# Prompt attention of a hybrid decoder step: other points of the projection for transposes, softmax and values, and the next input made two points later

## The chip, the cores and the metric

The kernel runs on one core of one Trainium2 chip. Time is device time in microseconds; lower is better. TensorE (PE) multiplies, VectorE (DVE) and ScalarE (ACT) read its results out of PSUM, GpSimd (POOL) helps out and issues some of the transfers, SyncE (SP) issues the rest.

## The reference

One layer of a decoder on 2048 prompt positions and 32 sample positions, width 1024, float32. What the change touches is the prompt's token mixing: one input projection, then two kinds of windowed attention on its columns.

```python
qa, ka, va, qb, kb, vb, ga, gb = _project(x, w_in)          # x @ w_in
qa, ka, qb, kb = _rope(qa, pos), _rope(ka, pos), _rope(qb, pos), _rope(kb, pos)
# A: 8 query heads on 2 key heads, window 128, blocks of 128, a learned sink per head
s = _band_scores(qa.reshape(...), ka, A_WINDOW)
p = _sink_softmax(s, _sink_logits(sink_a))
oa = _band_values(p, va)
# B: three groups of 4 heads, (window, dilation) = (128,1), (512,4), (2048,16)
for g, (win, dil) in enumerate(B_DIL):
    qg, kg, vg = (_stride_split(z[:, :, hs], dil) for z in (qb, kb, vb))
    p, lse = _softmax_lse(_band_scores(qg, kg, win // dil))
    outs.append(_band_values(p, vg))
# then: merge of the groups, gates, output projection, layer norm, gated ConvFFN, layer norm
```

Band scores of a block of 128 queries run over the keys of its own block and of the one before it.

## The kernel before

The program has three phases: projection with attention (to about 1320 us of the span), gates with output projection (to about 1710), and the ConvFFN. The change lies in the first.

**Precision.** Every float32 operand of a product is split in a high and a low part (`split`: ACT copies the high part, DVE or POOL subtracts to get the low one), and a product is three matmuls.

**Slots.** Phase 1 is a list `seq` of slots. The kinds are B0, B1, B2 (the three groups of B), A, and G (gates). Each kind has 16 slots of 128 prompt positions and one for the samples (slot 16; it comes last except in G). B0 and A take positions in order, B1 with stride 4, B2 with stride 16. In B2, and in every fourth slot of B1, a block has no block before it, so it has 128 keys and not 256.

**Points.** A slot multiplies its input `xs` (128 positions, both parts, eight k) with four units of weights of 256 columns, in two halves of two units; each half fills one PSUM tile `psd` of a pool with two tiles. After each half of a unit, that is after 12 matmuls of line 379, `adv()` lets every running attention job take one step: eight points a slot, numbered 0 to 7 here. The jobs are generators; each `yield` ends a step. The attention of a block starts in the slot after its projection. So the order of the program is written by hand, by where the `yield`s stand, and every engine works its instructions off in that order.

**Around the points.** `late()` reads the q/k half out of PSUM at point 5 in B and point 4 in A (`rope`: L425, L426, L433 on DVE), and the other half at the end of the slot (the gate's columns on ACT, L449). `prep` makes the input of the next slot: in B0 it loads and transposes x (L335) and copies it to `R` (L336 on ACT); in all it splits `xs` out of `R` (L41 on ACT, then L42 on DVE, or on POOL in A). It stands after unit 0, that is after point 1 (in the first slot of B0, B1 and B2 after point 3). `adv_bg` gives DVE a pair of instructions for the samples' scores (L797, L800) after point 2 and after point 6 in B; there are 16 such pairs for each group: in slots 2 to 9 of B1 and of B2, and from slot 2 to slot 13 of A. `adv_w` splits new weights near a change of kind.

**A job of B** (`attn_b`) transposes q (L630) and k (L634), splits them (`split_q`, `split_k`), splits v out of the PSUM tile (`split_v`), makes scores (`qk`, L617 and L619), the softmax of two pairs of heads (`softmax_pair`: maxima L546 on DVE, `nm` L550, exponentials L552 on ACT), transposes P (`transpose_p`, L562, then its split), multiplies with the values (L659) and adds the two parts of the result (`both`: L570 on ACT, L571 on DVE). A job of A (`attn_a`) does the same for two halves r of its heads.

Of the kernel before, what the change touches and what calls it, by code (L numbers as in the profile page):

```python
# [34 lines left out]
class Net:  # L35
# [254 lines left out]
    def adv(self):  # L290
        for j in self.jobs[::-1]:
            try:
                next(j)
            except StopIteration:
                self.jobs.remove(j)
# [56 lines left out]
    def slot(self, kind, i, t, xs, units, prep, after_unit, rp):  # L352
# [13 lines left out]
        for half in range(2):  # L366
            ps = self.pd.tile([128, 512], F32, tag="d", name="psd")
            for uu in range(2):
# [20 lines left out]
                if u == (1 if kind[0] == "B" and i == 0 else 0):  # L389
# [151 lines left out]
    def softmax_pair(self, sps, nk, mask, m, nm, den, cols, accum=True, init=None):  # L541
# [8 lines left out]
        nc.vector.tensor_scalar(nm[:, csl], m[:, csl], -SCALE, None, ALU.mult)  # L550
# [71 lines left out]
    def attn_b(self, kind, i, t):  # L622
# [6 lines left out]
        for p in range(2):  # L629
            nc.tensor.transpose(ps[:, p * 128:(p + 1) * 128], q[:, p * 128:(p + 1) * 128], self.idn)  # L630
        qT = self.split_q(ps[:, 0:256].rearrange("p (r t) -> p r t", r=2))
        ps = self.psO.tile([128, 512], F32, tag="o", name="pst")
        for p in range(2):
            nc.tensor.transpose(ps[:, p * 128:(p + 1) * 128], kv[:, p * 128:(p + 1) * 128], self.idn)  # L634
        self.split_k(ps[:, 0:256].rearrange("p (r t) -> p r t", r=2), i % 2)
        yield
        v = self.split_v(self.vps)
        vprev, self.vprev = self.vprev, v
        yield
# [4 lines left out]
        nc.gpsimd.dma_start(self.d_md[g, rows, :], md)  # L644
        yield
        vs = [v] if nb == 1 else ([v, vprev] if swap else [vprev, v])
        PTs = []
        yield
        for x in range(2):
            yield  # L650
            PTs.append(self.transpose_p(Ps[x], [(c, b) for c in range(2) for b in range(nb)]))
        O = self.buf()
        for x in range(2):
            yield
# [11 lines left out]
    def attn_a(self, t):  # L666
# [15 lines left out]
        yield  # L682
        m = self.at.tile([128, 8], F32, tag="m8", name="m8")
# [5 lines left out]
        def softmax(r, x, sps):  # L689
# [8 lines left out]
            nc.vector.tensor_scalar(nm[:, c:c + 2], m[:, c:c + 2], -SCALE, None, ALU.mult)  # L698
# [11 lines left out]
        def values(r, x, PT):  # L710
            for b in range(nb):
                for q in range(2):
                    nc.tensor.matmul(ops[:, r * 256:(r + 1) * 256], lhsT=vs[b][:, x], rhs=PT[:, q, b * 256:(b + 1) * 256],
                                     start=(b == 0 and q == 0), stop=(b == nb - 1 and q == 1))

        def out(x):
            o = self.both(O, ops, x)
            nc.gpsimd.dma_start(self.d_oa[x * 256:(x + 1) * 256, rows].rearrange("(h d) t -> d h t", h=4),
                                o.rearrange("p (h t) -> p h t", h=4))
# [913 lines left out]
```

## Time and profile before

| | us |
|---|---|
| median of 3 runs | 3258.62 (3256.92 to 3259.58) |
| profiled execution | 3259.99 |
| its span | 3258.2 |
| mean granted TensorE clock | 0.994 |

The page gives busy time by engine, waits by who waited for whom, and groups of instructions; times are microseconds from the span's start. A row of the timeline has start, length, engine, line, operation, output and inputs, and in brackets the idle time before it with what ended it. Matmuls overlap in the pipeline, so the distance from start to start says what one costs, not its own length. In the tables by stage the columns are: length, busy time of PE, PEld (weight loads), DVE, ACT and POOL with their counts, granted clock, share of the DMA engines and GB/s.

### The profile page before, as it was taken

The numbers are of one execution on the slowest core, as the hardware profiler recorded it, in microseconds if no ns is written. First come the engines' busy times: TensorE is split into PE (matmuls) and PEld (weight loads), VectorE is DVE, ScalarE is ACT, GpSimd is POOL, SyncE is SP. The second block draws the span as 40 slices with busy tenths as digits, with TensorE's granted clock in tenths as the row PEclk, the third lists the DMA queues.
The fourth block names the chain that finished last, engine by engine and source line by source line (L and its number), as shares of the span: only waits on it lengthen the run. The fifth ranks groups of instructions, "written<-read, shape, count | busy, mean of one in ns | idle before, by whom it ended". The sixth has DMA issues, their size and how long they took to land.

```text
span 3258.2 us, 56718 instructions
## 1 busy us (share of the span) xinstructions
PE 3175.0 (97%) x21839; PEld 2907.4 (89%) x21839; DVE 1947.6 (60%) x4030; ACT 1397.0 (43%) x3097; POOL 565.5 (17%) x671
## 2 busy tenths in 40 slices
PE   8999999999999899899999999999999999999999
PEld 8998999999899899788877988888888888999998
DVE  5667877877887632577765444564446444574446
ACT  6666656665666533412224243342243332342332
POOL 2112112223121200255540000030002100030001
PEclk9999999999999999999999999999999999999999
DMA  3113212412221343876744323443334423443231
GB/s 116 56 47 95 82 31 86 121 63 89 79 57 38 91 131 98 227 194 175 187 131 140 121 84 101 127 142 91 95 100 120 139 86 101 120 138 91 69 95 57
DMA packets 480036, 343.02 MB, mean 105 GB/s; under 512 B 113938, under 2 KB 435564, under 8 KB 479766
## 3 DMA queue, kind: packets, MB, share of 16 engines
q1 hardware_dynamic: 462390, 290.78, 31.5%
q0 software_dynamic: 17232, 48.56, 4.8%
q8 instruction: 172, 2.82, 0.4%
q14 instruction: 98, 0.80, 0.1%
q10 hardware_dynamic: 144, 0.07, 0.0%
HBM read 279.71 MB, written 59.59 MB: 104 GB/s over the span
## 4 chain that ended last, share of the span: by engine, by line
PE 58%; issue 2%; DMA 2%; DVE 1%; SPq 0%; ACT 0%; POOL 0%; DVEq 0%; POOLq 0%; ACTq 0%
PE psu L1392 31%; PE psdn L1070 14%; PE psw L1070 5%; PE psb L1070 4%; PE psd L379 2%; PE psdf L1070 1%; DMA oa<-d_oa 1%; PE pst L1234 0%; PE pso L964 0%; PE pst L1269 0%; DMA ob<-d_ob 0%; DMA ga<-d_gate 0%; DMA b<-in_w_o 0%; SPq L1126 0%; DMA b<-in_w_br_b 0%
## 5 line engine op out<-in xcount | busy, mean ns | idle before, releaser
L1392 PE MATMUL psu<-h,w 128*128 128x512 f32 (+1 forms) x5280 | 1013.6, 354 | 2.2 <-ACT h L41 2.0
L379 PE MATMUL psd<-w,xs 128*128 128x256 f32 x7680 | 1001.1, 285 | 8.7 <-ACT w L41 4.0
L1392 PEld LDWEIGHTS psu<-h,w 128*128 128x128 f32 x5280 | 861.2, 188 | 149.0 <-ACT h L41 3.4
L379 PEld LDWEIGHTS psd<-w,xs 128*128 128x128 f32 x7680 | 945.7, 190 | 12.9 <-ACT w L41 4.4
L1070 PE MATMUL psdn<-w,gt 128*128 128x256 f32 (+1 forms) x4008 | 474.9, 279 | 2.2 <-DVE y L1443 2.2
L1070 PEld LDWEIGHTS psdn<-w,gt 128*128 128x128 f32 (+1 forms) x4008 | 472.2, 186 | 5.3 <-DVE y L1443 4.5
L42 DVE TENSOR_TENSOR w<-b,w 128x512 fp32r<-128x512 f32 (+1 forms) x613 | 403.7, 717 | 21.4 <-ACT w L41 20.4
L41 ACT ACTIVATE w<-b 128x512 fp32r<-128x512 f32 x636 | 346.5, 607 | 127.4 <-PE psdn L1070 64.2
L1403 ACT ACTIVATE ext<-psu 128x512 f32<-128x512 f32 (+1 forms) x110 | 56.3, 512 | 452.2 <-PE psu L1392 452.1
L1416 DVE SCALAR_TENSOR_TENSOR ac<-ext,cw,ac 128x512 f32<-128x512 f32 (+1 forms) x88 | 71.1, 808 | 286.9 <-ACT ac L1415 286.9
L1443 DVE SCALAR_TENSOR_TENSOR y<-y,psdn 128x256 f32<-128x256 f32 x176 | 73.2, 420 | 274.2 <-PE psdn L1070 270.4
L1070 PE MATMUL psw<-WO,mT 128*128 128x512 f32 (+1 forms) x800 | 189.4, 395 | 0.9 <-DVE mT L42 0.9
L1070 PEld LDWEIGHTS psw<-WO,mT 128*128 128x128 f32 (+1 forms) x800 | 148.5, 186 | 38.9 <-DVE mT L42 1.1
L1412 POOL COPY mix<-ext 128x2 f32<-128x2 f32 x66 | 13.0, 196 | 926.5 <-ACT ext L1403 906.4
L42 DVE TENSOR_TENSOR xs<-R,xs 128x1024 fp32r<-128x1024 f32 x64 | 104.8, 1638 | 114.9 <-ACT xs L41 114.8
L1070 PE MATMUL psb<-w,oT 128*128 128x512 f32 (+1 forms) x600 | 147.6, 404 | 7.7 <-ACT b L449 5.0
L41 ACT ACTIVATE gt<-ac 128x512 fp32r<-128x512 f32 x110 | 58.3, 549 | 222.2 <-DVE ac L1423 162.7
L1070 PEld LDWEIGHTS psb<-w,oT 128*128 128x128 f32 (+1 forms) x600 | 112.4, 190 | 36.3 <-ACT b L449 5.7
L552 ACT ACTIVATE P<-P,nm 128x256 f32<-128x256 f32 (+1 forms) x192 | 86.4, 451 | 123.1 <-issue 87.4
L42 DVE TENSOR_TENSOR PT<-pst,PT 128x512 fp32r<-128x512 f32 (+1 forms) x160 | 96.2, 608 | 66.6 <-ACT PT L41 66.0
L662 POOL TENSOR_TENSOR b<-b 64x256 f32<-64x256 f32 x96 | 71.3, 742 | 337.4 <-DVE b L571 337.4
L41 ACT ACTIVATE xs<-R 128x1024 fp32r<-128x1024 f32 x80 | 116.2, 1452 | 0.9 <-ACT b L756 0.4
(257 smaller groups left out, 3679.1 us busy)
## 6 DMA issues: line engine op xcount, KB each, us to landing
b<-in_w_up SPq DMA_DIRECT2D x352, 256.0 KB, 3.9
b<-in_w_down SPq DMA_DIRECT2D x160, 256.0 KB, 3.4
b<-in_w_in SPq DMA_DIRECT2D x80, 256.0 KB, 4.1
b<-in_x_prompt SPq DMA_DIRECT2D x64, 256.0 KB, 4.0
b<-in_cache_b SPq DMA_DIRECT2D x64, 256.0 KB, 3.3
ga<-d_gate SPq DMA_DIRECT2D x32, 512.0 KB, 5.4
b<-d_q SPq DMA_DIRECT2D x48, 256.0 KB, 3.9
d_gate<-b SPq DMA_DIRECT2D x64, 128.0 KB, 1.9
```

What stands on the lines that cost most here:

```text
L41: self.nc.scalar.activation(hi, src, AF.Copy)
L42: (eng or self.nc.vector).tensor_tensor(lo, src, hi.bitcast(F32), ALU.subtract)
L379: nc.tensor.matmul(dst, lhsT=l, rhs=r[:, k, :], start=(k == 0 and q == 0), stop=(k == 7 and q == len(ops) - 1))
L552: nc.scalar.activation(P[:, x, :nk], P[:, x, :nk], AF.Exp, bias=nm[:, c:c + 1], scale=SCALE, accum_out=den[:, c:c + 1])
L662: nc.gpsimd.tensor_tensor(o[:, :, 0], o[:, :, 0], o[:, :, 1], ALU.add)
L1070: self.nc.tensor.matmul(ps[:x.shape[1]], lhsT=x, rhs=w, start=(first and q == 0), stop=(last and q == len(ops) - 1))
L1392: nc.tensor.matmul(ps[:, :b1 - b0], lhsT=w[:, k, c0:c0 + 128], rhs=h[:, x, k, b0:b1], start=(k == 0 and q == 0), stop=(k == 7 and q == 2))
L1403: nc.scalar.activation(ext[:, 2 + b0:2 + e1], ps[:, 0:e1 - b0], AF.Copy)
L1412: nc.gpsimd.tensor_copy(carry[:, j, :], ext[:, W:W + 2])
L1416: nc.vector.scalar_tensor_tensor(ac[:, :L], ext[:, 1:1 + L], cw[:, 1, j:j + 1], ac[:, :L], ALU.mult, ALU.add)
L1443: nc.vector.scalar_tensor_tensor(y[x][:M, cs], y[x][:M, cs], ALPHA if first else 1.0, ps[:M], ALU.mult, ALU.add)
```

## The change

The order in which jobs take their step is turned round: the older job first. The steps move:

- B: q and k are transposed into one PSUM tile at point 0 (k was in the one tile of pool `psO`); v is split at point 2 and not 1; scores and softmax come at point 3 and not 2; both P are transposed at point 0 of the slot after (they had points 5 and 6), directly ahead of the new block's q and k; both value products come at point 2 of that slot (they had point 7 and point 0).
- A: first scores and softmax at point 3 and not 2, P's transposes in pairs at point 5 and at point 0 of the next slot (they had points 4, 6, 9 and 8), values for half the heads at point 7 and at point 2 of the next slot, in one PSUM tile each; the result goes out in four transfers a slot and not two, of half the size.
- `prep` stands after unit 1, that is after point 3, in all prompt slots of B and A.
- `nm` (the maxima times -SCALE) is made by ACT and not by DVE.

Three places show how it moves instructions. DVE in a slot of B1 without a pair for the samples (row `ISA P` is one maximum, `ISA md` its read-out; `vr` is the split of v, `PT` the split of P). Before:

```order
L443 TENSOR_TENSOR vr<-psd,vr 128x2x64 x2
L42 TENSOR_TENSOR xs<-R,xs 128x1024
L546 ISA P,md<-pss,mk 128x256
...
L550 TENSOR_SCALAR nm<-md 128x2
L42 TENSOR_TENSOR PT<-pst,PT 128x512
L425 TENSOR_TENSOR q<-psd,cs 128x256
L425 TENSOR_TENSOR kv<-psd,cs 128x256
L426 TENSOR_TENSOR b<-psd,cs 128x512
```

After:

```order
L443 TENSOR_TENSOR vr<-psd,vr 128x2x64 x2
L546 ISA P,md<-pss,mk 128x256
...
L546 ISA md 128x1
L42 TENSOR_TENSOR xs<-R,xs 128x1024
L425 TENSOR_TENSOR q<-psd,cs 128x256
L425 TENSOR_TENSOR kv<-psd,cs 128x256
L426 TENSOR_TENSOR b<-psd,cs 128x512
L433 TENSOR_TENSOR q<-q,b 128x256
L433 TENSOR_TENSOR kv<-kv,b 128x256
L42 TENSOR_TENSOR PT<-pst,PT 128x512 x2
```

The split of xs stood ahead of the four maxima; now it stands behind them, directly ahead of the rotation that reads `psd`, and both splits of P follow the rotation. ACT in a slot of B0, before:

```order
L570 ACTIVATE b<-pso 64x512
L440 ACTIVATE vr<-psd 128x2x64 x2
L336 ACTIVATE R<-pst 128x4x128 x2
L41 ACTIVATE xs<-R 128x1024
L552 ACTIVATE P,md<-P,nm 128x256 x4
L41 ACTIVATE PT<-pst 128x512 x2
```

After:

```order
L570 ACTIVATE b<-pso 64x512 x2
L440 ACTIVATE vr<-psd 128x2x64 x2
L550 ACTIVATE nm<-md 128x2
L552 ACTIVATE P,md<-P,nm 128x256 x2
L550 ACTIVATE nm<-md 128x2
L552 ACTIVATE P,md<-P,nm 128x256 x2
L336 ACTIVATE R<-pst 128x4x128 x2
L41 ACTIVATE xs<-R 128x1024
```

The copies to R and the high part of xs moved behind the exponentials, and nm came in ahead of each pair. PE in a slot of B0, from the first block of a slot on, before:

```order
L379 MATMUL psd<-w,xs 128x256 x12
L630 MATMUL pst<-idn,q 128x128 x2
L634 MATMUL pst<-idn,kv 128x128 x2
L659 MATMUL pso<-PT,vr 128x256 x4
L379 MATMUL psd<-w,xs 128x256 x12
L335 MATMUL pst<-idn,b 128x128 x8
L379 MATMUL psd<-w,xs 128x256 x12
```

After:

```order
L562 MATMUL pst<-idn,P 128x128 x8
L630 MATMUL pst<-idn,q 128x128 x2
L630 MATMUL pst<-idn,kv 128x128 x2
L379 MATMUL psd<-w,xs 128x256 x24
L655 MATMUL pso<-PT,vr 128x256 x8
L379 MATMUL psd<-w,xs 128x256 x12
L617 MATMUL pss<-kH_378,qT 128x256
```

All twelve transposes of P, q and k stand together behind the first block, the eight value products two blocks later, and the scores one block after these. The diff (context cut):

```diff
@@ -288,7 +288,7 @@
                 self.bgq.pop(0)
 
     def adv(self):
-        for j in self.jobs[::-1]:
+        for j in list(self.jobs):
             try:
                 next(j)
             except StopIteration:
@@ -386,7 +386,7 @@
                         self.adv_w(pace[2 * u + kh])
                     if (u, kh) == (1, 0) or ((u, kh) == (3, 0) if kind != "A" else (u, kh) == (2, 0) and i < 6):
                         self.adv_bg()
-                if u == (1 if kind[0] == "B" and i == 0 else 0):
+                if u == (0 if kind == "G" or smp else 1):
                     out = prep()
                     if kind == "G" and i == 14:
                         rp.close()
@@ -547,7 +547,7 @@
                 out=P[:, x, :nk], in0=sps[:, x * 256:x * 256 + nk], in1=mask, scale=1.0,
                 scalar=NEG if init is None else init[:, c:c + 1], op0=ALU.add, op1=ALU.max, accum_out=m[:, c:c + 1])
         csl = slice(cols[0], cols[1] + 1, cols[1] - cols[0])
-        nc.vector.tensor_scalar(nm[:, csl], m[:, csl], -SCALE, None, ALU.mult)
+        nc.scalar.activation(nm[:, csl], m[:, csl], AF.Copy, scale=-SCALE)
         for x, c in enumerate(cols):
             nc.scalar.activation(P[:, x, :nk], P[:, x, :nk], AF.Exp, bias=nm[:, c:c + 1], scale=SCALE,
                                  accum_out=den[:, c:c + 1])
@@ -626,32 +626,28 @@
         sl, mask, nb, swap = self.keys(i, has_prev)
         nk = nb * 128
         ps = self.psT.tile([128, 512], F32, tag="t", name="pst")
-        for p in range(2):
-            nc.tensor.transpose(ps[:, p * 128:(p + 1) * 128], q[:, p * 128:(p + 1) * 128], self.idn)
+        for p in range(4):
+            nc.tensor.transpose(ps[:, p * 128:(p + 1) * 128], (q, kv)[p // 2][:, p % 2 * 128:(p % 2 + 1) * 128], self.idn)
         qT = self.split_q(ps[:, 0:256].rearrange("p (r t) -> p r t", r=2))
-        ps = self.psO.tile([128, 512], F32, tag="o", name="pst")
-        for p in range(2):
-            nc.tensor.transpose(ps[:, p * 128:(p + 1) * 128], kv[:, p * 128:(p + 1) * 128], self.idn)
-        self.split_k(ps[:, 0:256].rearrange("p (r t) -> p r t", r=2), i % 2)
+        self.split_k(ps[:, 256:512].rearrange("p (r t) -> p r t", r=2), i % 2)
+        yield
         yield
         v = self.split_v(self.vps)
         vprev, self.vprev = self.vprev, v
+        vs = [v] if nb == 1 else ([v, vprev] if swap else [vprev, v])
         yield
         md = self.at.tile([128, 8], F32, tag="m8", name="md")
         nm = self.at.tile([128, 8], F32, tag="nm", name="nm")
         sps = self.qk(qT, sl, nk, ((0, 0), (1, 1)))
         Ps = [self.softmax_pair(sps[x], nk, mask, md[:, 0:4], nm, md[:, 4:8], (x, 2 + x)) for x in range(2)]
         nc.gpsimd.dma_start(self.d_md[g, rows, :], md)
-        yield
-        vs = [v] if nb == 1 else ([v, vprev] if swap else [vprev, v])
-        PTs = []
-        yield
-        for x in range(2):
+        for _ in range(5):
             yield
-            PTs.append(self.transpose_p(Ps[x], [(c, b) for c in range(2) for b in range(nb)]))
+        PTs = [self.transpose_p(P, [(c, b) for c in range(2) for b in range(nb)]) for P in Ps]
+        yield
+        yield
         O = self.buf()
         for x in range(2):
-            yield
             ops = self.psT.tile([128, 512], F32, tag="t", name="pso") if x else self.psO.tile([128, 512], F32, tag="o", name="pso")
             for c in range(2):
                 for b in range(nb):
@@ -680,6 +676,7 @@
         self.split_k(pk[:, None, 0:128], i % 2)
         yield
         yield
+        yield
         m = self.at.tile([128, 8], F32, tag="m8", name="m8")
         nm = self.at.tile([128, 8], F32, tag="nm", name="nm")
         den = self.denA[:, i]
@@ -695,7 +692,7 @@
                 nc.vector.tensor_tensor_reduce(out=P[:, y, :nk], in0=sps[x][:, y * 256:y * 256 + nk], in1=mask, scale=1.0,
                                                scalar=self.sk8[:, c + y:c + y + 1], op0=ALU.add, op1=ALU.max,
                                                accum_out=m[:, c + y:c + y + 1])
-            nc.vector.tensor_scalar(nm[:, c:c + 2], m[:, c:c + 2], -SCALE, None, ALU.mult)
+            nc.scalar.activation(nm[:, c:c + 2], m[:, c:c + 2], AF.Copy, scale=-SCALE)
             for y in range(2):
                 nc.scalar.activation(P[:, y, :nk + 1], P[:, y, :nk + 1], AF.Exp, bias=nm[:, c + y:c + y + 1], scale=SCALE,
                                      accum_out=den[:, c + y:c + y + 1])
@@ -707,44 +704,35 @@
         def trans(P):
             return self.transpose_p(P, [(y, b) for b in range(nb) for y in range(2)])
 
-        def values(r, x, PT):
-            for b in range(nb):
-                for q in range(2):
-                    nc.tensor.matmul(ops[:, r * 256:(r + 1) * 256], lhsT=vs[b][:, x], rhs=PT[:, q, b * 256:(b + 1) * 256],
-                                     start=(b == 0 and q == 0), stop=(b == nb - 1 and q == 1))
-
-        def out(x):
-            o = self.both(O, ops, x)
-            nc.gpsimd.dma_start(self.d_oa[x * 256:(x + 1) * 256, rows].rearrange("(h d) t -> d h t", h=4),
-                                o.rearrange("p (h t) -> p h t", h=4))
+        def values(r, PTs):
+            ops = self.psO.tile([128, 512], F32, tag="o", name="pso")
+            for x in range(2):
+                for b in range(nb):
+                    for q in range(2):
+                        nc.tensor.matmul(ops[:, x * 256:(x + 1) * 256], lhsT=vs[b][:, x],
+                                         rhs=PTs[x][:, q, b * 256:(b + 1) * 256],
+                                         start=(b == 0 and q == 0), stop=(b == nb - 1 and q == 1))
+            o = self.both(self.buf(), ops, r)
+            for x in range(2):
+                h0 = (4 * x + 2 * r) * 64
+                nc.gpsimd.dma_start(self.d_oa[h0:h0 + 128, rows].rearrange("(y d) t -> d y t", y=2),
+                                    o[:, x * 256:(x + 1) * 256].rearrange("p (y t) -> p y t", y=2))
 
         sps = scores(0)
-        P0, P1 = softmax(0, 0, sps), softmax(0, 1, sps)
-        yield
-        yield
-        t0 = trans(P0)
+        Ps = [softmax(0, x, sps) for x in range(2)]
+        yield
+        yield
+        PTs = [trans(P) for P in Ps]
         sps = scores(1)
-        P0 = softmax(1, 0, sps)
-        yield
-        ops = self.psO.tile([128, 512], F32, tag="o", name="pso")
-        values(0, 0, t0)
-        yield
-        t0 = trans(P0)
-        yield
-        P0 = softmax(1, 1, sps)
-        yield
-        values(1, 0, t0)
-        O = self.buf()
-        out(0)
-        t0 = trans(P1)
-        yield
-        t1 = trans(P0)
-        yield
-        ops = self.psO.tile([128, 512], F32, tag="o", name="pso")
-        values(0, 1, t0)
-        yield
-        values(1, 1, t1)
-        out(1)
+        Ps = [softmax(1, x, sps) for x in range(2)]
+        yield
+        yield
+        values(0, PTs)
+        yield
+        PTs = [trans(P) for P in Ps]
+        yield
+        yield
+        values(1, PTs)
 
     def store_rec(self):
```

## The prediction

> **What bounds the kernel now.** I read the page first, then busy time by stage, then one slot of each kind on TensorE (PE), VectorE (DVE) and ScalarE (ACT), and last the granted clock around PE's longest waits.
>
> ```profile
> PE 3175.0 (97%) x21839; PEld 2907.4 (89%) x21839; DVE 1947.6 (60%) x4030; ACT 1397.0 (43%) x3097; POOL 565.5 (17%) x671
> ```
>
> PE is the bound, so only what PE waits for counts. The change touches the attention slots alone. The next table has four stretches that begin and end with a slot: slots 1 to 14 of B0, then slots 1 to 15 of B1, of B2 and of A. Columns: length, PE, weight loads, DVE, ACT and POOL busy, clock, DMA.
>
> ```profile
> 28.25:244.00 215.75, 215.75 (x1846) 215.14 (x1845) 133.57 (x363) 132.65 (x335) 36.25 (x53) 1.00 0.18 54
> 291.04:522.11 231.07, 220.98 (x1824) 214.14 (x1825) 172.34 (x421) 136.83 (x330) 40.53 (x60) 1.00 0.20 59
> 553.63:768.26 214.63, 209.17 (x1738) 204.16 (x1739) 159.64 (x422) 128.73 (x341) 46.73 (x72) 1.00 0.29 89
> 796.96:1080.48 283.52, 275.46 (x2201) 259.60 (x2200) 224.10 (x579) 171.69 (x517) 54.07 (x44) 1.00 0.22 60
> ```
>
> B0 has no idle PE at all; B1, B2 and A have 10.1, 5.5 and 8.1 us, and DVE is at 62 to 79%. So there is little to win, and DVE is the engine to watch. One B0 slot on PE; starts are in the first column:
>
> ```profile
> 213.07 1.58 PE L379 MATMUL psd<-w,xs 128*128 128x256 f32 x12
> ...
> 216.85 1.04 PE L335 MATMUL pst<-idn,b 128*128 128x128 f32 x8
> 217.65 1.66 PE L379 MATMUL psd<-w,xs 128*128 128x256 f32 x12
> 219.15 0.40 PE L617 MATMUL pss<-kH,qT 128*128 128x256 f32 x2
> ...
> 220.10 4.42 PE L379 MATMUL psd<-w,xs 128*128 128x256 f32 x36
> 224.35 0.60 PE L562 MATMUL pst<-idn,P 128*128 128x128 f32 x4
> 224.71 1.66 PE L379 MATMUL psd<-w,xs 128*128 128x256 f32 x12
> ...
> 228.07 0.63 PE L659 MATMUL pso<-PT,vr 128*128 128x256 f32 x4
> 228.53 1.59 PE L379 MATMUL psd<-w,xs 128*128 128x256 f32 x12
> ```
>
> From start to start: slot 15.46 us; 36 products 4.25, so one takes 0.118 and a block of 12 takes 1.42; eight score products 0.95; four value products 0.46; eight transposes 0.80, four 0.36: about 0.1 each in a burst of either size. A burst therefore costs by its transposes, not by its edges, and merging bursts gives PE nothing. DVE and ACT in the slot before it:
>
> ```profile
> 202.62 0.69 DVE L571 TENSOR_TENSOR b<-pso,b 64x512 f32<-64x512 f32 x1
> 203.34 0.49 DVE L443 TENSOR_TENSOR vr<-psd,vr 128x128 fp32r<-128x128 f32 x2
> 204.99 1.23 DVE L42 TENSOR_TENSOR xs<-R,xs 128x1024 fp32r<-128x1024 f32 x1 [1.15 <-ACT xs L41]
> 206.13 0.42 DVE L546 CUSTOM_DVE_ANT_0 P<-pss,mk 128x256 f32<-128x256 f32 x1
> ...
> 206.93 0.17 DVE L550 TENSOR_SCALAR nm<-md 128x2 f32<-128x2 f32 x1
> ...
> 210.76 0.41 DVE L425 TENSOR_TENSOR q<-psd,cs 128x256 f32<-128x256 f32 x1
> ...
> 211.43 0.68 DVE L426 TENSOR_TENSOR b<-psd,cs 128x512 f32<-128x512 f32 x1
> ```
> ```profile
> 202.76 1.10 ACT L336 ACTIVATE R<-pst 128x512 f32<-128x512 f32 x2
> 203.89 1.06 ACT L41 ACTIVATE xs<-R 128x1024 fp32r<-128x1024 f32 x1
> 207.13 0.51 ACT L552 ACTIVATE P<-P,nm 128x256 f32<-128x256 f32 x1 [2.18 <-DVE nm L550]
> ...
> 208.63 0.49 ACT L552 ACTIVATE P<-P,nm 128x256 f32<-128x256 f32 x1
> ...
> 213.27 0.59 ACT L570 ACTIVATE b<-pso 64x512 f32<-64x512 f32 x1 [1.29 <-PE pso L659]
> ```
>
> Today the next slot's input xs is done by 206.2, 8.6 us into a slot that began 15.46 before 213.07, ahead of the softmax, and the rotation of the q/k half (L425, L426) has its columns read by 212.11. Both beat the slot's end at 213.07, by 7 and by 1 us.
>
> **The step that decides: xs behind the softmax.** After the change DVE's queue holds, in a B slot: maxima of the four score rows, then xs, then L425 and L426. ACT's holds: exponentials, (B0: the copies R), then xs. And the first product of the next slot writes the PSUM tile that L425 and L426 read, since that pool has two tiles, one for each half. So a chain runs from the scores of one slot to the start of the next. I add it up, with S the slot's start.
>
> PE: four blocks 5.68, one burst of 12 transposes 1.31, the eight values 0.95, the eight scores 0.95: the scores end at S+8.9. ACT saw products 0.20 after their end (213.07 to 213.27), so DVE starts the maxima at S+9.1; the value sums and vr ahead of them (2 x 0.69 behind ACT's 0.59, then 0.49) are through by S+8.7. Then: first pair of maxima 0.80 (206.13 to 206.93); two nm on ACT, not seen before, taken at 0.25 each with their waits, since the DVE form took 0.17 to 0.2 up to the exponential (bounds 0.15 and 0.45); four exponentials at 0.50. ACT is free at S+12.4. B0: R 1.13, xs high part 1.10, xs low part on DVE 1.14, the reads of L425 and L426 1.35, and 0.06 to PE: the next slot starts at **S+17.1**, where PE alone would need 15.4. B0: 12 slots by 1.65, two early ones with smaller softmax by 0.75, slot 15 (its xs is strided) by 2.4: **+23.7**.
>
> In B1 and B2, xs reads R with a stride:
>
> ```profile
> 466.39 2.07 ACT L41 ACTIVATE xs<-R 128x1024 fp32r<-128x1024 f32 x1
> ...
> 468.49 2.03 DVE L42 TENSOR_TENSOR xs<-R,xs 128x1024 fp32r<-128x1024 f32 x1 [1.03 <-ACT xs L41]
> ```
> ```profile
> 321.05 0.68 DVE L797 TENSOR_TENSOR b<-b 128x512 f32<-128x512 f32 x1
> ...
> 321.77 0.69 DVE L800 TENSOR_REDUCE S<-b 128x8 f32<-128x512 f32 x1
> ```
> ```profile
> 648.72 0.28 DVE L546 CUSTOM_DVE_ANT_0 P<-pss,mk 128x128 f32<-128x128 f32 x1
> ...
> 651.07 0.36 ACT L41 ACTIVATE PT<-pst 128x256 fp32r<-128x256 f32 x1
> ```
>
> B1: S+12.4, xs 2.1 and 1.95, reads 1.35: S+17.9. In slots 2 to 9 a pair for the samples (1.42) now stands ahead of the maxima, which start at S+10.1: S+18.9. Every fourth block has no previous block, which takes 0.9 off the slots it is in. Slots 1 to 15 sum to 269.6 against 231.1: **+38.5**. B2 has one key block: scores end at S+7.9, the softmax holds ACT 2.35 (648.72 to 651.07) plus 0.25; S+16.1, with a sample pair S+17.4. Eight slots of 17.4 and seven of 16.1 are 251.9 against 214.6: **+37.3**. In these slots PE needs 14.5 and 13.6, so it would stand idle 2.5 to 4.4 us each.
>
> **What idle PE does to the clock.**
>
> ```profile
> 1099.27:1102.68 3.41, 1.67 (x14) 1.46 (x13) 3.38 (x6) 1.87 (x5) 1.53 (x1) 1.00 0.52 157
> 269.84:273.25 3.41, 1.47 (x12) 1.10 (x10) 3.29 (x5) 3.36 (x8) 0.90 (x1) 1.00 0.25 65
> 273.26:276.67 3.41, 3.02 (x14) 2.73 (x13) 3.38 (x8) 0.95 (x2) 1.44 (x2) 0.50 0.48 144
> ```
> ```profile
> 272.55 0.74 PE L659 MATMUL pso<-PT,vr 128*128 128x256 f32 x4 [1.94 <-DVE PT L42]
> 273.24 2.89 PE L379 MATMUL psd<-w,xs 128*128 128x256 f32 x12
> ```
>
> A 3.41-us stretch with PE busy 1.47 was followed by one at half clock, where 12 products took 2.89 for 1.58; one with 1.67 was not. A half-speed stretch costs about 1.5 us of products, all ahead of the scores, so it lengthens the chain. Idle of 1.7 (B0) leaves 1.7 busy in any stretch: nothing, at the edge. B2's 2.5 falls into one stretch half the time: 0.8 a slot; 3.4 (B1 without samples) three times in four: 1.1; 3.8 to 4.4 always, and one in three twice: 2.0. Sum 16 x 2.0 + 7 x 1.1 + 7 x 0.8: **+45** (bounds 0 and 100: each slot twice at half clock). The Trainium skill ("TensorE: Matmul & The Clock Gate", Part 1 and its table of goals) puts the drop at an idle window of about 3.4 us, and asks for no gap over about 3. By that only the 16 slots with sample pairs would pay; the 1.94-us wait above speaks against it.
>
> **The rest.** Removed: the wait of the k transposes for the one psO tile, in rows of the kind 401.79 below; it is inside the slot lengths above. The maxima's factor nm leaves DVE; in A that is worth most, since there it could take 1.42 us for the 0.17 in B0.
>
> ```profile
> 401.79 0.44 PE L634 MATMUL pst<-idn,kv 128*128 128x128 f32 x2 [0.93 <-DVE b L571]
> ```
> ```profile
> 994.41 1.42 DVE L698 TENSOR_SCALAR nm<-m 128x2 f32<-128x2 f32 x1
> ```
> ```profile
> 985.33:1004.36 19.03, 18.68 (x151) 17.57 (x150) 15.22 (x40) 11.76 (x35) 3.67 (x3) 1.00 0.20 53
> ```
>
> A: xs's low part is on POOL, so DVE's rotation of q follows the first softmax at once and its PSUM tile is free in time. PE's work alone is 128 products by 0.118 and 21 transposes by 0.11, 17.4. The chain there is another one. The first scores end at S+9.0 (four blocks, 13 transposes, eight values, eight scores); as in B, ACT is through with the exponentials at S+12.8 (two copies of the sink more) and with xs at S+13.9; P1's transposes wait 0.7 for it, which moves the slot's end to S+18.1. P's two high parts (0.6) and the low parts on DVE (0.65) are ready at S+15.8, the second maxima at S+17.5, their exponentials at S+19.5, the sum behind them in both queues at S+20.7, and the rotation of k, last on DVE, at S+21.5. PE asks for k's transpose at 18.1 + 2.7 = S+20.8: 0.8 late, so the slot takes 18.9, against 19.03: **-2** in all. Bounds: -1.6 a slot (PE's work alone) and +1.5 (the second softmax one step later). POOL issues 32 more d_oa transfers of half the size. They stand ahead of xs's low part and wait for sums that end before the scores; POOL is busy 3.67 of the 19.03, so I cost them at nothing, and if that room were gone each microsecond would count 16 times. At the three changes of kind DVE carries 2 to 3 us more old work into the splits of new weights: **+7.5** (0 to 15). SP's loads move two points later with xs and are due a slot later: nothing. Phases 2 and 3 are unchanged.
>
> Sum: 23.7 + 38.5 + 37.3 + 45 - 2 + 7.5 = +150 us on the profiled execution's 3259.99 (1.8 beyond its span of 3258.2, 1.4 over the median 3258.62): **3410**.
>
> **Rivals.** (1) Faster, 0.05: xs and the rotation are in time after all, which needs the chain from the scores' end to the last read to be under 6.3 us in B0 and 5.4 in B1 instead of 8.0 and 8.8; nothing in the rows is that short. Then the slots come down to PE's work, 14.5 (13.9 for four of them), 13.6 and 17.4: 231.1 + 214.6 + 283.5 less 215, 204 and 261 is 49, so 3211. (2) The chain as worked out, but no half clock, 0.22: 3260 + 105 = 3365. (3) Half clock only where one idle time outlasts a whole 3.41-us stretch, 0.08: 16 x 2.0 for 45 gives 3397; this is the page's rule above. (4) A lengthens too, 0.13: if rotation of k is the last thing on DVE's crowded queue (79% busy), +1.5 a slot on 16: 3434. (5) Only the strided kinds stall, since B0's 1.65 is made of small terms, 0.07: 3350 with some half clock. The sum as it stands: 0.45.
>
> **Numbers.** The bounds of single terms (nm, clock, A, changes of kind) spread the main case by some 40 to either side, and (2) to (5) lie mostly within: 3345 to 3450. No change means within 0.2%, about what a measurement of this kernel can tell: faster 0.05, same 0.02, slower 0.93.
>
> **What would show it.** Right: PE's longest idle stands before the first product of a slot (L379), released by DVE's L426, 1.5 to 4 us; slots of 17 to 19 us in B0 and B1; xs on ACT directly behind the exponentials; the page's clock row below 9 in the slices of B1 and B2; the row of k's transposes without a wait for L571. Wrong: idle before L379 under 0.3 us, or PE waiting for PT or kL instead.

## The result, and the profile after

The change makes the kernel slower: 3419.33 us (median of 4 runs, 3416.7 to 3424.7) for 3258.57 before (4 runs, 3256.92 to 3259.58), a ratio of 1.0496 [1.0478, 1.0514]. The profiled execution took 3419.28, with a span of 3417.5 and a mean clock of 0.976. Lines of its page: busy time, the granted clock in 40 slices, and the group of the projection's products with the idle time ahead of them:

```profile
PE 3223.2 (94%) x21839; PEld 2962.8 (87%) x21839; DVE 1914.2 (56%) x3870; ACT 1422.0 (42%) x3257; POOL 587.0 (17%) x703
...
PEclk9999889988999999999999999999999999999999
...
L379 PE MATMUL psd<-w,xs 128*128 128x256 f32 x7680 | 1017.6, 290 | 135.8 <-DVE b L426 111.5
```

DVE has 33 us less to do than before and PE waits for it all the same: 111.5 us ahead of products, ended by L426, the last read of `psd`. The clock falls below 9 tenths in four slices, two in B1 and two in B2. The same four stretches as before the change (B0's slots 1 to 14, then slots 1 to 15 of B1, B2 and A; columns as there):

```profile
26.52:269.85 243.33, 220.60 (x1833) 217.96 (x1833) 129.74 (x334) 133.60 (x361) 36.37 (x53) 0.99 0.16 48
322.52:621.38 298.86, 244.46 (x1813) 239.64 (x1813) 170.60 (x389) 141.36 (x360) 40.58 (x60) 0.90 0.15 47
657.12:933.47 276.35, 231.70 (x1733) 227.12 (x1734) 157.34 (x389) 134.09 (x370) 46.93 (x72) 0.90 0.23 69
964.58:1241.96 277.38, 267.34 (x2206) 257.33 (x2205) 199.44 (x524) 180.94 (x578) 70.73 (x72) 1.00 0.23 61
```

B0 grew by 27.6 us here, B1 by 67.8 and B2 by 61.7; A shrank by 6.1. One slot of B0 on the timeline, from its start at 198.75 to the next slot's at 216.18; in brackets what an instruction waited for:

```profile
200.24 1.03 PE L562 MATMUL pst<-idn,P 128*128 128x128 f32 x8
...
201.47 3.08 PE L379 MATMUL psd<-w,xs 128*128 128x256 f32 x24
...
203.74 0.77 ACT L604 ACTIVATE kH<-pst 64x256 fp32r<-64x256 f32 x2 [1.12 <-DVE qT L591]
...
207.68 0.49 DVE L443 TENSOR_TENSOR vr<-psd,vr 128x128 fp32r<-128x128 f32 x2
...
208.09 0.41 DVE L546 CUSTOM_DVE_ANT_0 P<-pss,mk 128x256 f32<-128x256 f32 x1
...
208.89 0.20 ACT L550 ACTIVATE nm<-md 128x2 f32<-128x2 f32 x1 [2.01 <-DVE md L546]
...
211.36 1.06 ACT L336 ACTIVATE R<-pst 128x512 f32<-128x512 f32 x2
212.45 1.06 ACT L41 ACTIVATE xs<-R 128x1024 fp32r<-128x1024 f32 x1
213.54 1.23 DVE L42 TENSOR_TENSOR xs<-R,xs 128x1024 fp32r<-128x1024 f32 x1 [4.00 <-ACT xs L41]
...
214.69 0.42 DVE L425 TENSOR_TENSOR q<-psd,cs 128x256 f32<-128x256 f32 x1
...
215.35 0.68 DVE L426 TENSOR_TENSOR b<-psd,cs 128x512 f32<-128x512 f32 x1
...
216.18 1.66 PE L379 MATMUL psd<-w,xs 128*128 128x256 f32 x12 [1.76 <-DVE b L426]
```

The burst of 12 transposes takes 1.23 us (200.24 to 201.47), and PE waits nowhere but at the end of this slot. (In B1 and B2 it also waits 3.8 and 5.5 us in all, in mid-slot, for the split of v on DVE, L443, which the change moved from point 1 to point 2.) What follows is the forecast chain, link by link: maxima, nm, exponentials, R, xs on ACT, xs on DVE (which stood idle for 4.00 us behind the maxima), the reads of `psd`, PE. The slot is 17.43 long, forecast 17.1.

### The profile page after: what moved, and what is told of

The parts are those of the page before. It is cut to its first block, busy times and chain, and to the rows that moved or that the text cites. A ratio compares the mean times of both kernels' runs of the same rounds, so it can differ in the third digit from the quotient of the medians.

```text
span 3417.5 us, 56732 instructions
## 1 busy us (share of the span) xinstructions
PE 3223.2 (94%) x21839; PEld 2962.8 (87%) x21839; DVE 1914.2 (56%) x3870; ACT 1422.0 (42%) x3257; POOL 587.0 (17%) x703
## 4 chain that ended last, share of the span: by engine, by line
PE 58%; DMA 1%; DVE 1%; issue 1%; ACT 0%; POOL 0%; SPq 0%; DVEq 0%; ACTq 0%; POOLq 0%
PE psu L1380 29%; PE psdn L1058 14%; PE psw L1058 5%; PE psb L1058 4%; PE psd L379 4%; PE psdf L1058 1%; DMA oa<-d_oa 1%; PE pso L952 1%; PE pst L1222 0%; PE pst L1257 0%; DMA ob<-d_ob 0%; DVE w L42 0%; DMA b<-in_w_o 0%; DVE y L1431 0%; DMA b<-in_w_br_a 0%
## 5 line engine op out<-in xcount | busy, mean ns | idle before, releaser
L379 PE MATMUL psd<-w,xs 128*128 128x256 f32 x7680 | 1017.6, 290 | 135.8 <-DVE b L426 111.5
L379 PEld LDWEIGHTS psd<-w,xs 128*128 128x128 f32 x7680 | 969.8, 196 | 152.0 <-issue 118.3
L41 ACT ACTIVATE PT<-pst 128x512 fp32r<-128x512 f32 (+1 forms) x160 | 78.8, 533 | 211.7 <-PE pst L562 211.2
```

Of the source, the lines that this page charges most:

```text
L41: self.nc.scalar.activation(hi, src, AF.Copy)
L379: nc.tensor.matmul(dst, lhsT=l, rhs=r[:, k, :], start=(k == 0 and q == 0), stop=(k == 7 and q == len(ops) - 1))
```

## The experiments

The theory is that xs stands behind the softmax on ACT and DVE, the rotation behind xs, and the next slot's first product behind the rotation; PE's idle time then halves the clock. Its rivals: the new bursts, value points and order of jobs cost by themselves; the low clock is a symptom; nm on ACT is the cost.

| kernel | median us | ratio to the kernel before |
|---|---|---|
| changed kernel | 3419.33 | 1.0496 [1.0478, 1.0514] |
| rotation ahead of xs | 3335.08 | 1.0229 [1.0214, 1.0244] |
| xs and v back at point 1 | 3281.19 | 1.0061 [1.0046, 1.0076] |
| filler products in B1, B2 | 3384.26 | 1.0382 [1.0367, 1.0398] |
| kernel before, prep alone moved | 3283.43 | 1.0070 [1.0054, 1.0087] |
| nm on DVE again | 3395.79 | 1.0417 [1.0402, 1.0431] |
| k in psO again | 3430.16 | 1.0519 [1.0505, 1.0534] |
| k in a score tile | 3400.79 | 1.0435 [1.0421, 1.0450] |
| kernel before, A alone changed | 3253.65 | 0.9982 [0.9974, 0.9991] |
| xs, v, sample pair at point 1, k in psO | 3260.14 | 0.9999 [0.9990, 1.0009] |
| the same, k in a score tile, last block sooner | 3229.31 | 0.9911 [0.9897, 0.9924] |

**The rotation ahead of xs.**

```diff
-                if u == (0 if kind == "G" or smp else 1):
+                if u == (0 if kind == "G" or smp else 2 if kind[0] == "B" else 1):
```

> The changed kernel, with B's prep one unit later still (behind point 5), so that DVE reads the q/k half out of PSUM (L425, L426) ahead of the low part of xs, which now comes last. Theory (the next slot waits for a chain softmax, xs, rotation on DVE): the reads of 1.35 us leave the chain to xs, so the slots of B get about 1 to 1.35 us shorter, 45 such slots: -45 to -60, and with less idle PE 15 to 25 us less half clock: 3335 to 3360. PE's wait at a slot's start is then ended by xs (L42) and not by L426. Rival (the new order of bursts, values and jobs costs by itself, wherever xs stands): 3419 as the changed kernel, within 10.

It measured 3335.08, 84 us faster, at the fast end of what the theory gave. Its page has the link changed as the theory has it: PE now waits for xs itself.

```profile
L379 PE MATMUL psd<-w,xs 128*128 128x256 f32 x7680 | 1003.2, 287 | 78.8 <-DVE xs L42 36.9
```

B0's slots came to 16.46 from 17.44, B2's without a sample pair to 15.1 from 16.55. Nothing of the bursts, values or order of jobs was touched, so the rival that they carry the whole loss, wherever xs stands, falls here already. This run can't say what they do to the 76 us that are left.

**xs back where it was.**

```diff
-                if u == (0 if kind == "G" or smp else 1):
+                if u == (1 if kind[0] == "B" and i == 0 else 0 if kind[0] == "B" or kind == "G" or smp else 1):
...
         self.split_k(ps[:, 256:512].rearrange("p (r t) -> p r t", r=2), i % 2)
         yield
-        yield
         v = self.split_v(self.vps)
...
+        yield
```

> The changed kernel, with B's prep back behind point 1 and B's split of v back at point 1, as before the change; the one burst of transposes, the values two points later, the order of jobs, nm on ACT and all of A stay. Theory: xs is ready long before the slot's end again, so PE waits for no rotation; B0 about 15.4, B1 about 15.4 (16.8 with a pair for the samples, which stands ahead of the maxima), B2 14.1 (15.5): 3255 to 3275, that is at least 145 of the 161 us come back. Rival (bursts, values and order of jobs carry the loss): most of it stays, over 3360.

3281.19: 138 of the 161 us come back, a little short of the 145 expected. The edit moves two things, xs and the split of v, and no run moves one back without the other. Slots 1 to 14 of B0 and 1 to 15 of B1 and B2:

```profile
27.42:252.57 225.15, 217.72 (x1832) 215.18 (x1833) 129.41 (x334) 133.01 (x359) 35.76 (x52) 1.00 0.18 52
302.18:535.72 233.54, 215.89 (x1812) 213.48 (x1812) 168.62 (x389) 138.76 (x357) 43.42 (x59) 1.00 0.21 59
569.97:788.41 218.44, 206.34 (x1732) 204.12 (x1733) 156.38 (x390) 132.56 (x370) 50.50 (x72) 1.00 0.28 87
```

B1 and B2 are within 4 us of the times before the change. B0 is 9 us over them, and a row of its timeline, in the slot that starts at 171.97, shows why:

```profile
179.51 0.71 PE L655 MATMUL pso<-PT,vr 128*128 128x256 f32 x4 [0.42 <-DVE kL L608]
```

The second value tile comes from the pool of three that the transposes use, and with the transposes of x between them it falls on the tile of q and k, which kL (L608) reads last. PE loses some 0.6 us by it (1.05 us from the start of the first four value products to the start of the next four, where four take 0.46), and such slots take 16.1 for 15.47 before. The three sample slots at the ends of B0, B1 and B2 stay 9 us longer than before together.

**prep alone, in the kernel before.**

```diff
-                if u == (1 if kind[0] == "B" and i == 0 else 0):
+                if u == (0 if kind == "G" or smp else 1):
```

> The kernel before, with one thing alone taken from the change: prep stands behind point 3 in all prompt slots of B and A. Theory: here the softmax comes at point 2, so xs stands behind it as after the change, but scores and softmax come one point (1.4 us) sooner than in the changed kernel, so that only a part of the wait arises: B0 15.7, B1 16.5 (17.9 with a sample pair), B2 15.2 (16.6), in all +40 to +65: 3300 to 3325. Rival (bursts, values and order of jobs carry the loss): 3258 within 6.

3283.43, +24 where 40 to 65 was expected, and neither the theory's number nor the rival's. B0 stayed at 15.46 a slot, B1 rose by 9.4 us, B2 by 7.3, A by 6.2. Rows of its timeline, in a slot of B1 that starts at 454.10:

```profile
460.62 0.42 DVE L546 CUSTOM_DVE_ANT_0 P<-pss,mk 128x256 f32<-128x256 f32 x1
...
465.94 2.02 DVE L42 TENSOR_TENSOR xs<-R,xs 128x1024 fp32r<-128x1024 f32 x1 [3.46 <-ACT xs L41]
...
467.89 0.68 DVE L42 TENSOR_TENSOR PT<-pst,PT 128x512 fp32r<-128x512 f32 x1
...
469.97 1.31 PE L379 MATMUL psd<-w,xs 128*128 128x256 f32 x9 [0.61 <-DVE b L426]
```

The first maximum starts 6.5 us into the slot; in the changed kernel it is 9.3 (198.75 to 208.09). I had counted one block, 1.4 us. Of the other 1.4, about 1.3 is the transposes of P (0.80) and half of the values (0.46), which in the kernel before do not stand between the slot's start and the scores. Take 2.8 off the changed kernel's chains at full clock and B0 comes out at 14.6, under PE's own work, and a B1 slot without a pair at 15.3 (18.13 in the filler run below, less 2.8); with the 0.6 of the split of P that stands ahead of the rotation here, 15.9, and the measured slot is 15.88. (nm is on DVE here, which is worth 0.29 in a B0 slot below, so the working is good to some 0.3 us and not to the hundredth.) So neither half of the edit makes the loss by itself. xs moved alone costs 24 us (6 of it in A), the rest of the change with xs and v at their old points 22 (with 6 gained in A), all together 161: each uses up slack in the same chain, and the second one finds none. How much of the difference is v's was not tried; its split makes PE wait too, 13.0 us in 26 waits in the changed kernel and 21.9 in 41 with the rotation ahead of xs.

**Products of no use at the slots' ends.** They keep PE from standing idle for the whole wait.

```diff
+        nf = {"B1": (14, 22), "B2": (8, 16)}.get(kind, (0, 0))[2 <= i <= 9] if 1 < i < 15 else 0
+        if nf:
+            fl = self.psO.tile([128, 512], F32, tag="o", name="psf")
+            for x in range(nf):
+                nc.tensor.matmul(fl[:, 0:256], lhsT=xs[:, 0, 0, :], rhs=units[0][0][:, 0, :], start=(x == 0), stop=(x == nf - 1))
```

> The changed kernel, with products of no use put on PE at the end of each slot of B1 (14; 22 in slots 2 to 9) and of B2 (8; 16), slots 2 to 14, into a PSUM tile that nobody uses at that time; their results are read by nobody. They are about 1.6 to 2.6 and 0.9 to 1.9 us of work, less than PE's wait there. Theory of the clock (idle PE drops to half clock, and this lengthens the chain): the half-speed stretches in B1 and B2 go away and the kernel gets faster although PE does more: -35 to -45, 3375 to 3385, mean clock 0.99. Rival (the low clock falls on time in which PE waits anyway): 3419 within 6, whatever the clock.

3384.26: PE executes 414 matmuls more and the kernel is 35 us faster. B1 fell from 298.86 to 278.53 and B2 from 276.35 to 259.89, with the clock at 0.99 in both (the two stretches by stage):

```profile
322.25:600.78 278.53, 250.50 (x2058) 245.19 (x2058) 170.12 (x389) 139.24 (x360) 40.41 (x60) 0.99 0.18 50
636.47:896.36 259.89, 231.17 (x1900) 226.60 (x1900) 157.27 (x389) 132.12 (x370) 46.77 (x72) 0.99 0.25 73
```

The half-speed stretches are a cause, worth 36.8 us in B1 and B2 (20.3 and 16.5), since the half-speed products stand ahead of the scores in the chain.

**nm on DVE.**

```diff
-        nc.scalar.activation(nm[:, csl], m[:, csl], AF.Copy, scale=-SCALE)
+        nc.vector.tensor_scalar(nm[:, csl], m[:, csl], -SCALE, None, ALU.mult)
...
-            nc.scalar.activation(nm[:, c:c + 2], m[:, c:c + 2], AF.Copy, scale=-SCALE)
+            nc.vector.tensor_scalar(nm[:, c:c + 2], m[:, c:c + 2], -SCALE, None, ALU.mult)
```

> The changed kernel, with nm on DVE again (B and A). Theory: two nm on ACT cost 0.2 us each ahead of exponentials on the chain; on DVE the first one costs the same there, and the second runs beside the exponentials: -0.2 to -0.3 a B slot, 48 slots, -10 to -15 with a little clock; A within 1 us a slot (DVE is its full queue): up to +10. Together 3400 to 3425. Rival (nm on ACT is the change's real cost, since it puts a hand-over from DVE to ACT into every softmax): most of the 161 us comes back, below 3330.

3395.79, 24 us faster; the top of what was expected was 19. A B0 slot lost 0.29 (17.44 to 17.15), which is the expected size, and A came to 276.82 from 277.38. The rest is clock: B1's went to 0.94 and B2's to 0.95. As the real cost nm is ruled out, since 137 us of the loss stay.

**k's PSUM tile.** The rows of the changed kernel suggested why its B0 slot is 0.3 longer than forecast: q and k now share a tile, and ACT's kH waits 1.12 us for DVE's qT, which makes kL, the value sums and vr late; the first maximum then waits for vr (207.68 + 0.49), not for the scores.

```diff
+        pk = self.psO.tile([128, 512], F32, tag="o", name="pst")
...
-            nc.tensor.transpose(ps[:, p * 128:(p + 1) * 128], (q, kv)[p // 2][:, p % 2 * 128:(p % 2 + 1) * 128], self.idn)
+            nc.tensor.transpose((ps, pk)[p // 2][:, p % 2 * 128:(p % 2 + 1) * 128], (q, kv)[p // 2][:, p % 2 * 128:(p % 2 + 1) * 128], self.idn)
...
-        self.split_k(ps[:, 256:512].rearrange("p (r t) -> p r t", r=2), i % 2)
+        self.split_k(pk[:, 0:256].rearrange("p (r t) -> p r t", r=2), i % 2)
```

> The changed kernel, with one thing alone taken back: k is transposed into its own PSUM tile (pool psO) and not into q's. Reading: in the changed kernel ACT's copies kH wait 1.12 us for DVE's qT, which reads the same PSUM tile, and by this kL, vr and the first maximum are late; that is the 0.25 to 0.3 us by which a B0 slot is longer than forecast (17.44 for 17.1). Then kH starts at once, the B0 slot is 17.15, and the kernel 12 us shorter, with a few microseconds more where less idle PE saves a half-speed stretch: 3400 to 3410. Rival (the 0.3 us comes from elsewhere, ACT's queue of value sums before vr): 3419 within 5.

3430.16, 11 us slower where both readings expected no loss. Its timeline, in a B0 slot that starts at 185.06:

```profile
188.96 0.77 ACT L604 ACTIVATE kH<-pst 64x256 fp32r<-64x256 f32 x2
...
191.56 1.18 PE L656 MATMUL pso<-PT,vr 128*128 128x256 f32 x8 [0.69 <-DVE kL L608]
...
195.02 0.42 DVE L546 CUSTOM_DVE_ANT_0 P<-pss,mk 128x256 f32<-128x256 f32 x1
```

kH no longer waits, but the one tile of `psO` is also the values' first tile, so PE waits for kL there, and the maxima start 9.96 us into the slot and not 9.34. In the kernel before, the values that use this tile came at point 7, behind the scores, and so did not make the scores late. The edit replaced a wait by a longer one, so it said nothing on the first. The next one does: k in one of the two score tiles.

```diff
-        pk = self.psO.tile([128, 512], F32, tag="o", name="pst")
+        pk = self.psS.tile([128, 512], F32, tag="s", name="pst")
```

> The changed kernel, with k transposed into one of the two score tiles (pool psS, free at that point) and not into q's tile; psO stays with the values. In the run with k in psO the copies kH no longer waited for qT, but the value products waited 0.69 us for kL to free psO and the scores came 0.9 us later. Reading to test: with neither wait, kL and the value sums are about 0.8 us earlier, the first maximum is no longer held up by vr and starts 0.2 us behind the scores: B0 slots 17.15 to 17.2 for 17.44, B1 and B2 as much shorter, and a few half-speed stretches less: 3395 to 3410. Rival (the 0.3 us is not from there): 3419 within 5.

Its timeline, in a B0 slot that starts at 178.42:

```profile
186.86 0.49 DVE L443 TENSOR_TENSOR vr<-psd,vr 128x128 fp32r<-128x128 f32 x2
...
187.47 0.42 DVE L546 CUSTOM_DVE_ANT_0 P<-pss,mk 128x256 f32<-128x256 f32 x1
...
195.56 1.66 PE L379 MATMUL psd<-w,xs 128*128 128x256 f32 x12 [1.46 <-DVE b L426]
```

3400.79, and the B0 slot (178.42 to 195.56) is 17.14: the 0.29 is from there. In the profiled execution, at 3408.89 the slowest of the four, B1 gained 3.9 and B2 only 0.3 and not "as much". Their clock stayed at 0.90 and 0.89. A slot of B2 that met no half-speed stretch is 0.5 shorter (16.06 for 16.57, slot 13 in both), and more of B2's slots met one; so what the chain gave there was taken by where the half-speed stretches fell.

**A alone.** The kernel before with the changed `attn_a`, its place of prep, the order of jobs and nm on ACT, in A only (the order also in G, where A's last job ends):

```diff
+        self.older = kind in ("A", "G")
...
-        for j in self.jobs[::-1]:
+        for j in (list(self.jobs) if self.older else self.jobs[::-1]):
...
-                if u == (1 if kind[0] == "B" and i == 0 else 0):
+                if u == (1 if (kind[0] == "B" and i == 0) or (kind == "A" and not smp) else 0):
...
-        P0, P1 = softmax(0, 0, sps), softmax(0, 1, sps)
+        Ps = [softmax(0, x, sps) for x in range(2)]
...
```

> The kernel before, with the changed kernel's A alone: its attn_a, prep behind point 3 in A, older job first in A, nm on ACT in A; B as before. Theory (A's gain is its own): slots 1 to 15 of A at 277.4 us instead of 283.5, -5 to -7 in all: 3252 to 3254. Rival (A gained in the changed kernel only since the slots before it left less old work): 3259 within 3.

3253.65, a ratio of 0.9982 [0.9974, 0.9991], and A's gain is its own: its slots 1 to 15 take 277.09 where they took 283.52.

```profile
794.86:1071.95 277.09, 267.22 (x2205) 257.33 (x2204) 199.64 (x524) 180.24 (x577) 70.82 (x72) 1.00 0.23 61
```

**A version that is faster.** First xs, v and B's first sample pair at point 1, with k in `psO` (the edits for xs, v and k as above, and this one):

```diff
-                    if (u, kh) == (1, 0) or ((u, kh) == (3, 0) if kind != "A" else (u, kh) == (2, 0) and i < 6):
+                    if (u, kh) == ((1, 0) if kind == "A" else (0, 1)) or ((u, kh) == (3, 0) if kind != "A" else (u, kh) == (2, 0) and i < 6):
```

> The changed kernel with prep and v's split in B at point 1 as before (this alone gave 3281), k in its own PSUM tile, and the first sample pair of B at point 1, ahead of xs, and not at point 2, ahead of the maxima. Theory: the value products of B0 lose their 0.6-us wait for kL (14 slots, -8), and the 16 slots with a pair lose the 1.4 us by which the pair made the maxima late (-18 to -22); A keeps its gain: 3250 to 3258, at or a little under the kernel before. Rival (the pair now makes xs late and this PE): B1 and B2 slots with a pair stay at 16.4 and 15.3: 3272.

3260.14, the same as the kernel before and 2 us over what was expected. The pairs cost nothing now (B2's slots are 14.3 with and without), but the values wait for kL in `psO` again, 0.69 us in a slot of B1 and 1.65 in a sample slot, as two rows of the timeline show:

```profile
451.66 1.16 PE L656 MATMUL pso<-PT,vr 128*128 128x256 f32 x8 [0.69 <-DVE kL L608]
...
529.27 1.18 PE L656 MATMUL pso<-PT,vr 128*128 128x256 f32 x8 [1.65 <-DVE kL L608]
```

So k went to a score tile, and the last block of a group one point sooner:

```diff
-        pk = self.psO.tile([128, 512], F32, tag="o", name="pst")
+        pk = self.psS.tile([128, 512], F32, tag="s", name="pst")
...
-        yield
+        if i < 15:
+            yield
...
-        for _ in range(5):
+        for _ in range(5 if i < 15 else 6):
```

> The kernel that gave 3260 (prep and v at point 1, k apart, the pair at point 1), with k in a score tile and not in psO, and with the last block of each group of B making its scores one point sooner, in the slot of the samples. Theory: the value products lose their 0.85-us wait for kL in B1 and their 1.8 us in the three sample slots, and softmax and reading of psd there come 0.9 us sooner: -8 in B1, -8 in the sample slots: 3243 to 3250, under both kernels. Rival (these waits lay beside others that stay): 3258 within 3.

The page's group of the products, and by stage slots 1 to 15 of B1 and of B2:

```profile
L379 PE MATMUL psd<-w,xs 128*128 128x256 f32 x7680 | 977.6, 284 | 20.0 <-DVE b L495 10.0
```
```profile
289.13:506.92 217.79, 214.66 (x1812) 213.34 (x1812) 167.45 (x389) 138.71 (x355) 40.04 (x59) 1.00 0.22 63
539.56:743.00 203.44, 203.16 (x1730) 203.19 (x1731) 154.80 (x391) 133.14 (x371) 47.13 (x72) 1.00 0.32 94
```

3229.31, 0.9% faster than the kernel before, and 31 us under the run before it where 10 to 17 was expected. B1 gave 11.8 of this (229.63 to 217.79), the three sample slots 6.1, and B2 9.6 (213.06 to 203.44), which I had left out although its values waited for kL too (6.7 us in 14 slots). B2 now has next to no idle PE (13.62 a slot, PE's own work), and B1 0.2 us a slot.

## Why the prediction was right, and where its terms were off

The forecast was 3410, the time 3419.33, and the likeliest case is the one that happened: the wait stands where the prediction put it, before a slot's first product, ended by L426, behind the chain that it names. That the sum came so close is in part luck, since the chain was 21 us too short in the forecast and clock, A and the rest together 11.5 too long. Its terms against the span's growth of 159.3 us (3258.2 to 3417.5):

| term | forecast | measured | how |
|---|---|---|---|
| B0, chain | +23.7 | +27.6 | slots 1 to 15, +30.2 (slot 15 went from 15.46 to 18.11), less 2.6 for two slots that met a half-speed stretch |
| B1, chain | +38.5 | +47.5 | 67.8 less 20.3, which the filler run gave back |
| B2, chain | +37.3 | +45.2 | 61.7 less 16.5, likewise |
| clock | +45 | +39.4 | 2.6 + 20.3 + 16.5 |
| A | -2 | -6.1 | the rows above |
| the rest | +7.5 | +5.7 | what is left; the three sample slots at the ends alone are +10.7 |

The filler run's clock is 0.99 and not 1.00, so the clock's true share is a little larger and the chain's a little smaller.

The chain was mis-sized by 21 us in 45 slots, in two places. The step that "the value sums and vr ahead of them ... are through by S+8.7" is the first that failed: vr ended at S+9.4, since kH waits for qT in the tile that q and k now share, a part of the change whose cost I had not counted. With that wait gone the slot is the forecast's (17.15 for 17.1; the forecast's own terms add up to 17.18, not 17.1); 0.29 in 45 slots, taken as the same in all, is 13 us. And the sample pair, which I put in a gap between vr and the maxima, found no gap: it cost 1.64 us a slot (filler run: 19.77 for 18.13 in B1, 18.18 for 16.55 in B2), where I had 1.0 and 1.3; in 16 slots that is 8 us.

nm on ACT was right: 0.20 a piece in the rows, inside the bounds, and a B0 slot is 0.29 shorter in the run with both on DVE. The burst of transposes has no edges to pay for, as said, and A's 32 more transfers, costed at nothing, left A shorter than forecast.

The clock was 39 for 45, near in sum and less so in its parts: B0, costed at nothing, paid 2.6 in two slots, and of B2's last five slots, which have no pair and were costed at 0.8 each, one paid, 1.6. Rival (1), faster, fell with the time, and rival (2), no half clock, by the filler run. Rival (3), half clock only behind the longest waits, gave 3397; B1's slots without a pair go against it, as the last section shows. Rival (4), A longer, and (5), only strided kinds, fell by the stretches of A and B0.

A's steady slot was right within 0.03 us (18.9 forecast, 18.87 measured in slots 7 to 13, 19.02 before). Both of its waits are there: from start to start PE loses 1.0 us at P's second transposes (1161.00 to 1162.44 in slot 11) and 0.5 at k's, forecast 0.7 and 0.8. But I set it against one slot of 19.03 and took that for all. Slots 3 to 6 took 19.7 before and 18.9 now, and the last two 18.3. What failed in this term is the choice of one slot to stand for all: the mean of the stretch, 18.90, hid four long slots and two short early ones.

What I had not seen is that the loss is joint. I priced the chain as it stood after the whole edit, which was enough for the time. But I then expected 40 to 65 us of xs alone, and the run of prep alone showed 24.

## What to carry to other kernels

When work moves on an in-order queue, add up the whole chain from the last input to the release of the buffer that the next stage needs, and compare its length with the stage: parts of a change that each cost little can use the same slack, here 24 us for xs alone, 22 for the rest without xs and v, and 161 for the whole. An operation that nothing waits for soon (here the next input, made two points later) still holds up what is queued behind it, so place it by what follows it and not by its own due time. Before giving a transpose its own PSUM tile, look who else uses that pool: k's own tile lost 11 us in one pool and won 19 in another.

## What the runs showed of the hardware

The granted clock goes by fixed stretches of 3.413 us: the half-speed ones of the changed kernel begin at 129.13, 525.08 and 750.36, which are 116 and 66 stretches apart. By stretch, each here with the one after it (for the last, the two after it), and then one row of PE's timeline:

```profile
125.72:129.12 3.40, 1.64 (x14) 1.52 (x13) 2.53 (x6) 0.39 (x1) 0.00 (x0) 1.00 0.43 136
129.13:132.53 3.40, 3.40 (x18) 3.40 (x17) 1.38 (x2) 1.79 (x4) 0.00 (x0) 0.50 0.21 73
521.66:525.07 3.41, 1.34 (x12) 1.14 (x10) 2.79 (x4) 0.97 (x2) 0.00 (x0) 1.00 0.13 40
525.08:528.48 3.40, 2.81 (x13) 2.84 (x14) 1.20 (x3) 0.00 (x0) 0.00 (x0) 0.50 0.08 24
746.94:750.35 3.41, 0.73 (x7) 0.52 (x5) 2.57 (x4) 1.43 (x3) 0.00 (x0) 1.00 0.23 53
750.36:753.76 3.40, 2.69 (x12) 2.72 (x13) 2.61 (x5) 0.00 (x0) 0.54 (x1) 0.50 0.71 219
753.77:757.17 3.40, 3.40 (x17) 3.40 (x17) 1.48 (x4) 1.53 (x4) 0.00 (x0) 0.50 0.53 179
```
```profile
525.67 2.90 PE L379 MATMUL psd<-w,xs 128*128 128x256 f32 x12 [2.66 <-DVE b L426]
```

PE busy 1.34 and even 1.64 of 3.41 us was followed by half speed; the 1.67 shown in the prediction was not. So how much of a fixed stretch PE works counts, and in these rows the edge lies a little under half. But it is not sharp by this measure: in the same run a stretch with PE busy 1.58 (668.43 to 671.84) was not followed by half speed, and one with 2.09, at the end of B2 (938.09 to 941.50), was. What else decides there stays open.

An idle gap by itself doesn't decide either. PE's longest idle time within the stretch was 1.8 us in the one with 1.58 and 1.0 in the one with 2.09. The waits in the rows at 125.72 and 521.66 were 1.76 and 2.66 us. The Trainium skill ("TensorE: Matmul & The Clock Gate", table of goals) asks for no gap over about 3 us, and these two lie under that. The same page of the Trainium skill speaks in Part 1 of a free-running window of about 3.4 us, which agrees with the grid here.

Of the 13 waits of 1.5 to 1.95 us in B0 two met such a stretch, of six of 1.8 to 2.1 in B2 one; the waits of 2.2 to 4.3 in B1 and of 3.4 in B2 all did, while one of 2.69 at the end of B0 (before 287.93) met none. In the rows from 746.94 on, the second stretch, idle for 0.7 of its 3.4 us, did not bring the clock back, so a third followed at half speed. One such stretch ahead of the scores made a slot 1.3 us longer in B0 (18.77 for 17.44) and 1.6 in B2 (18.12 for 16.56).
